# Sharing the last row of a ReLU-mean between two engines, with running sums and the scaling on GpSimd

## Chip, cores, metric

One core of a Trainium2 chip. The metric is the device time of one execution in microseconds; a profile's span is about 1.8 us shorter than that time (163.1 against 164.88 us for the kernel before).

## The reference

```python
x: float32 [32, 512, 1024]
out = np.mean(np.maximum(x, 0), axis=-1)      # float32 [32, 512]
```

67.1 MB are read and 64 KB written. Seen from the core, it is 128 partitions with 128 rows of 1024 values each.

## The kernel before

The rows are taken in eight tiles of 16 rows (8.4 MB each), three buffers deep. Even rows go to ScalarE, odd rows to VectorE. Each engine does ReLU and row sum in one instruction with an accumulator output; the profile lists the read-out of that accumulator as an instruction of its own (`DVE_READ_ACCUMULATOR` on VectorE). The last tile arrives in shrinking pieces (8, 4, 2, 1 rows, then row 15 of the tile in 512, 256 and 256 columns), so that little work is left after the last bytes. That tail is what the change rewrites:

```python
def dve_row(nc, src, acc):
    nc.vector.tensor_scalar(out=src, in0=src, scalar1=0.0, scalar2=None,
                            op0=ALU.max, op1=ALU.add, accum_out=acc)
...
def finish(lo, hi):                       # scaling by 1/1024
    nc.vector.tensor_scalar_mul(out=res[:, lo + 1:hi:2], in0=sum_v[:, lo + 1:hi:2], scalar1=inv)   # L73
    nc.scalar.mul(out=res[:, lo:hi:2], in_=sum_a[:, lo:hi:2], mul=inv)                             # L74
...
finish(0, j0)                             # 112 columns, before the last tile's rows
...                                       # rows 0 to 13 of the last tile
finish(j0, j0 + lo)                       # 14 columns
act_row(nc, xt[:, lo, :D // 2], part_a[:, 0:1])          # row 14, halves
dve_row(nc, xt[:, lo, D // 2:], part_v[:, 0:1])
act_row(nc, last[:, :D // 4], part_a[:, 1:2])            # row 15, first quarter
dve_row(nc, last[:, D // 4:D // 2], part_v[:, 1:2])      # second quarter
nc.vector.tensor_scalar(res[:, J - 2] = (part_a0 + part_v0) * inv)       # L106, row 14 (abridged)
dve_row(nc, last[:, D // 2:3 * D // 4], part_v[:, 2:3])  # third quarter
nc.vector.tensor_scalar(part_v1 = part_v1 + part_a1 + part_v2)           # L111 (abridged)
dve_row(nc, last[:, 3 * D // 4:], part_v[:, 3:4])        # last quarter
nc.vector.tensor_scalar(res[:, J - 1] = (part_v3 + part_v1) * inv)       # L116 (abridged)
nc.sync.dma_start(out=outr, in_=res)
```

In the compiled program, L106 stands ahead of the second quarter.

Of the kernel before, what the change touches and what calls it, by code (L numbers as in the profile page):

```python
# [1 line left out]

# [4 lines left out]

F32 = mybir.dt.float32
ALU = mybir.AluOpType
RELU = mybir.ActivationFunctionType.Relu  # L10


def act_row(nc, src, acc):

    nc.scalar.activation(out=src, in_=src, func=RELU, accum_out=acc)  # L15


def dve_row(nc, src, acc):

    nc.vector.tensor_scalar(  # L20
        out=src, in0=src, scalar1=0.0, scalar2=None,
        op0=ALU.max, op1=ALU.add, accum_out=acc,
    )


@with_exitstack
def kernel(
    ctx: ExitStack,
    tc: tile.TileContext,
    x: bass.AP,  # L30
    out: bass.AP,
):
    nc = tc.nc
    P = nc.NUM_PARTITIONS
    xf = x.flatten_outer_dims()
    R, D = xf.shape
    assert R % P == 0
    J = R // P
    inv = 1.0 / D
    xr = xf.rearrange("(p j) d -> p j d", p=P, j=J)  # L40
    outr = out.flatten().rearrange("(p j) -> p j", p=P, j=J)

    NB = 16
    BUFS = 3
    full = J // NB - 1

    row_pieces = []
    left = NB
    while left > 1:
        row_pieces.append(left // 2)  # L50
        left -= left // 2
    col_pieces = [D // 2, D // 4, D // 4]

    in_pool = ctx.enter_context(tc.tile_pool(name="in", bufs=BUFS))
    res_pool = ctx.enter_context(tc.tile_pool(name="res", bufs=1))
    sum_a = res_pool.tile([P, J], F32)
    sum_v = res_pool.tile([P, J], F32)
    res = res_pool.tile([P, J], F32)
    part_a = res_pool.tile([P, 2], F32)
    part_v = res_pool.tile([P, 4], F32)  # L60

    def rows(xt, lo, n, j0):

        for k in range(lo, lo + n):
            j = j0 + k
            if j % 2:
                dve_row(nc, xt[:, k, :], sum_v[:, j:j + 1])
            else:
                act_row(nc, xt[:, k, :], sum_a[:, j:j + 1])

    def finish(lo, hi):

        nc.vector.tensor_scalar_mul(out=res[:, lo + 1:hi:2], in0=sum_v[:, lo + 1:hi:2], scalar1=inv)  # L73
        nc.scalar.mul(out=res[:, lo:hi:2], in_=sum_a[:, lo:hi:2], mul=inv)  # L74

    for t in range(full):
        j0 = t * NB
        xt = in_pool.tile([P, NB, D], F32, name="xt")
        nc.sync.dma_start(out=xt, in_=xr[:, j0:j0 + NB, :])  # L79
        rows(xt, 0, NB, j0)  # L80

    j0 = full * NB
    xt = in_pool.tile([P, NB, D], F32, name="xt")
    lo = 0
    for n in row_pieces:
        nc.sync.dma_start(out=xt[:, lo:lo + n, :], in_=xr[:, j0 + lo:j0 + lo + n, :])  # L86
        lo += n
    c = 0
    for w in col_pieces:
        nc.sync.dma_start(out=xt[:, lo, c:c + w], in_=xr[:, j0 + lo, c:c + w])  # L90
        c += w

    finish(0, j0)
    lo = 0
    for n in row_pieces[:-1]:
        rows(xt, lo, n, j0)
        lo += n
    finish(j0, j0 + lo)


    last = xt[:, NB - 1, :]
    act_row(nc, xt[:, lo, :D // 2], part_a[:, 0:1])
    dve_row(nc, xt[:, lo, D // 2:], part_v[:, 0:1])
    act_row(nc, last[:, :D // 4], part_a[:, 1:2])
    dve_row(nc, last[:, D // 4:D // 2], part_v[:, 1:2])
    nc.vector.tensor_scalar(  # L106
        out=res[:, J - 2:J - 1], in0=part_a[:, 0:1], scalar1=part_v[:, 0:1], scalar2=inv,
        op0=ALU.add, op1=ALU.mult,
    )
    dve_row(nc, last[:, D // 2:3 * D // 4], part_v[:, 2:3])  # L110
    nc.vector.tensor_scalar(  # L111
        out=part_v[:, 1:2], in0=part_v[:, 1:2], scalar1=part_a[:, 1:2], scalar2=part_v[:, 2:3],
        op0=ALU.add, op1=ALU.add,
    )
    dve_row(nc, last[:, 3 * D // 4:], part_v[:, 3:4])
    nc.vector.tensor_scalar(  # L116
        out=res[:, J - 1:J], in0=part_v[:, 3:4], scalar1=part_v[:, 1:2], scalar2=inv,
        op0=ALU.add, op1=ALU.mult,
    )
    nc.sync.dma_start(out=outr, in_=res)  # L120


# [1 line left out]
_INS = ['x']  # L124
_OUTS = [((32, 512), 'float32')]


# [23 lines left out]
```

## Time and profile before

| | |
|---|---|
| time, median of 3 | 164.88 us (164.87 to 165.01) |
| span of the profile | 163.1 us |
| share of the chain that ended last | input transfers 83%, VectorE 14% |
| last landing of row 15's third piece | 159.19 us |
| issue of the output transfer | 160.67 us |
| between the two ("the stretch") | 1.48 us |
| issue to the end of the span | 2.43 us |

Up to the landing, the stream decides; after the issue, the output transfer and the program's close decide. A change of the tail can act only between the two. This kernel was profiled once, so its 1.48 us rest on one execution. The landings are read from the trace's records of the transfers' completion semaphores: the moment at which the last of sixteen increments arrives. The lines of the profile are shown in the prediction.

### The profile page before, as it was taken

To read this page: it belongs to the slowest core of one execution; us is meant where nothing else is said; L and a number is where in the kernel's file an instruction comes from. 1 tells how busy PE (TensorE), PEld (TensorE's weight loads), DVE (VectorE), ACT (ScalarE), POOL (GpSimd) and SP (SyncE) were. 2 spreads that over 40 slices of the span, in tenths; PEclk is the share of its full clock that TensorE was granted. 3 is DMA by queue.
4 is the path that set the end of the run, shared out by engine and by line. 5 is a ranking of instruction groups with operands and counts; after the bars stand their busy time and mean duration, and the time that the engine had idled before them with its cause. 6 is when DMAs were issued, how large, how long until landed. Compare 5 with 4: busy or idle time off the path is not lost.

```text
span 163.1 us, 351 instructions
## 1 busy us (share of the span) xinstructions
DVE 75.4 (46%) x139; ACT 69.4 (43%) x133; POOL 0.2 (0%) x4
## 2 busy tenths in 40 slices
DVE  0000039900596008940099202990059700799993
ACT  3000039700594008920099002980059500797890
POOL 0000000000000000000000000000000000000000
DMA  7979989989998998997997998998998897999970
GB/s 257 482 321 482 482 354 450 514 354 418 514 418 354 514 418 354 514 482 305 498 484 340 466 498 354 434 514 370 402 514 386 386 514 338 434 442 394 409 298 16
DMA packets 2162, 67.19 MB, mean 412 GB/s; under 512 B 240, under 2 KB 624, under 8 KB 880
## 3 DMA queue, kind: packets, MB, share of 16 engines
q1 hardware_dynamic: 2160, 67.18, 96.0%
q14 instruction: 2, 0.02, 0.0%
HBM read 67.11 MB, written 0.07 MB: 412 GB/s over the span
## 4 chain that ended last, share of the span: by engine, by line
DMA 83%; DVE 14%; SPq 1%; issue 0%; DVEq 0%
DMA xt<-in_x_dram 83%; DVE xt L20 13%; SPq L86 0%; SPq L79 0%; DVE part_v L111 0%; DVE res L116 0%; DVE res L106 0%; DVE res L73 0%; DVEq L20 0%; DVEq L111 0%; DVEq L106 0%
## 5 line engine op out<-in xcount | busy, mean ns | idle before, releaser
L20 DVE TENSOR_SCALAR_CACHE_REDUCE xt<-xt 128x1024 f32<-128x1024 f32 (+1 forms) x67 | 74.4, 1172 | 84.9 <-DMA xt<-in_x_dram 84.8
L15 ACT ACTIVATE xt<-xt 128x1024 f32<-128x1024 f32 (+1 forms) x65 | 66.7, 1027 | 88.9 <-DMA xt<-in_x_dram 88.9
L15 ACT ACTIVATION_READ_ACCUMULATOR xt<-xt 128x1 f32 x65 | 12.1, 187 | 0.0
L20 DVE DVE_READ_ACCUMULATOR xt<-xt 128x1 f32 x67 | 5.6, 83 | 0.0
L15 ACT ACT_TABLE_LOAD x1 | 1.3, 1283 | 0.7 <-PEq L135 0.7
L74 ACT ACTIVATE res<-sum_a 128x56 f32<-128x56 f32 (+1 forms) x2 | 0.5, 232 | 0.1
L73 DVE TENSOR_SCALAR res<-sum_v 128x56 f32<-128x56 f32 (+1 forms) x2 | 0.4, 184 | 0.1
L111 DVE TENSOR_SCALAR part_v<-part_v,part_a 128x1 f32<-128x1 f32 x1 | 0.3, 273 | 0.1
L106 DVE TENSOR_SCALAR res<-part_a,part_v 128x1 f32<-128x1 f32 x1 | 0.2, 214 | 0.1
L116 DVE TENSOR_SCALAR res<-part_v 128x1 f32<-128x1 f32 x1 | 0.2, 214 | 0.0
L135 POOL MEMSET const-uint8-127<- 128x1 uint8 x1 | 0.1, 102 | 0.0
L135 POOL MEMSET const-bfloat16-1.0<- 128x1 bf16 x1 | 0.1, 101 | 0.0
L135 POOL MEMSET const-float32-0.0<- 128x1 f32 x1 | 0.1, 98 | 0.2 <-issue 0.2
L135 POOL MEMSET const-float32-1.0<- 128x1 f32 x1 | 0.1, 98 | 0.0
## 6 DMA issues: line engine op xcount, KB each, us to landing
xt<-in_x_dram SPq DMA_DIRECT2D x1, 4096.0 KB, 39.0
xt<-in_x_dram SPq DMA_DIRECT2D x1, 2048.0 KB, 43.5
xt<-in_x_dram SPq DMA_DIRECT2D x1, 1024.0 KB, 45.5
xt<-in_x_dram SPq DMA_DIRECT2D x1, 512.0 KB, 46.3
xt<-in_x_dram SPq DMA_DIRECT2D x1, 256.0 KB, 46.5
xt<-in_x_dram SPq DMA_DIRECT2D x2, 128.0 KB, 42.7
xt<-in_x_dram SPq DMA_DIRECT2D x7, 48.9
out_dram<-res SPq DMA_DIRECT2D x1, 64.0 KB, 1.6
```

The lines of the kernel that those rows point to most:

```text
L15: nc.scalar.activation(out=src, in_=src, func=RELU, accum_out=acc)
L20: nc.vector.tensor_scalar(out=src, in0=src, scalar1=0.0, scalar2=None, op0=ALU.max, op1=ALU.add, accum_out=acc,)
L73: nc.vector.tensor_scalar_mul(out=res[:, lo + 1:hi:2], in0=sum_v[:, lo + 1:hi:2], scalar1=inv)
L74: nc.scalar.mul(out=res[:, lo:hi:2], in_=sum_a[:, lo:hi:2], mul=inv)
L106: nc.vector.tensor_scalar(out=res[:, J - 2:J - 1], in0=part_a[:, 0:1], scalar1=part_v[:, 0:1], scalar2=inv, op0=ALU.add, op1=ALU.mult,)
L111: nc.vector.tensor_scalar(out=part_v[:, 1:2], in0=part_v[:, 1:2], scalar1=part_a[:, 1:2], scalar2=part_v[:, 2:3], op0=ALU.add, op1=ALU.add,)
L116: nc.vector.tensor_scalar(out=res[:, J - 1:J], in0=part_v[:, 3:4], scalar1=part_v[:, 1:2], scalar2=inv, op0=ALU.add, op1=ALU.mult,)
L135: nc = _bacc.Bacc("TRN2", target_bir_lowering=False, num_devices=1)
```

## The change

Its intent: shorten what VectorE does after the last bytes. ScalarE gets half of the third quarter; VectorE's pieces of row 15 hand their sum on as the start value of the next; the scalings of finished rows and row 14's combination go to GpSimd.

```diff
-def dve_row(nc, src, acc):
+def dve_row(nc, src, acc, init=None):
-        out=src, in0=src, scalar1=0.0, scalar2=None,
+        out=src, in0=src, scalar1=0.0, scalar2=init,
...                                    # one tile `sums` in place of sum_a, sum_v; one tile `part`
     def finish(lo, hi):
-        nc.vector.tensor_scalar_mul(out=res[:, lo + 1:hi:2], in0=sum_v[:, lo + 1:hi:2], scalar1=inv)
-        nc.scalar.mul(out=res[:, lo:hi:2], in_=sum_a[:, lo:hi:2], mul=inv)
+        nc.gpsimd.tensor_scalar(
+            out=res[:, lo:hi], in0=sums[:, lo:hi], scalar1=inv, scalar2=0.0, op0=ALU.mult, op1=ALU.add,
+        )
...
+    nc.gpsimd.tensor_scalar(            # L98: row 14's combination, was L106 on VectorE
+        out=res[:, J - 2:J - 1], in0=part[:, 0:1], scalar1=part[:, 1:2], scalar2=inv, op0=ALU.add, op1=ALU.mult,
+    )
+    act_row(nc, last[:, :256], part[:, 2:3])
+    dve_row(nc, last[:, 256:512], part[:, 3:4])
+    nc.gpsimd.tensor_scalar(            # L103
+        out=part[:, 4:5], in0=part[:, 2:3], scalar1=inv, scalar2=0.0, op0=ALU.mult, op1=ALU.add,
+    )
+    act_row(nc, last[:, 512:640], part[:, 5:6])
+    dve_row(nc, last[:, 640:768], part[:, 6:7], init=part[:, 3:4])
+    nc.scalar.activation(               # L108
+        out=part[:, 7:8], in_=part[:, 5:6], func=ACT.Identity, scale=inv, bias=part[:, 4:5],
+    )
+    dve_row(nc, last[:, 768:], part[:, 8:9], init=part[:, 6:7])
+    nc.vector.scalar_tensor_tensor(     # L112
+        out=res[:, J - 1:J], in0=part[:, 8:9], scalar=inv, in1=part[:, 7:8], op0=ALU.mult, op1=ALU.add,
+    )
```

More of the change, by code (lines that the diff above doesn't have):

```diff
@@ L9 @@
 ALU = mybir.AluOpType
-RELU = mybir.ActivationFunctionType.Relu
+ACT = mybir.ActivationFunctionType
 def act_row(nc, src, acc):
-    nc.scalar.activation(out=src, in_=src, func=RELU, accum_out=acc)
-def dve_row(nc, src, acc):
+    nc.scalar.activation(out=src, in_=src, func=ACT.Relu, accum_out=acc)
+def dve_row(nc, src, acc, init=None):
     nc.vector.tensor_scalar(
-        out=src, in0=src, scalar1=0.0, scalar2=None,
+        out=src, in0=src, scalar1=0.0, scalar2=init,
         op0=ALU.max, op1=ALU.add, accum_out=acc,
@@ L41 @@
     outr = out.flatten().rearrange("(p j) -> p j", p=P, j=J)
+    xlast = xr[:, J - 1, :]
     NB = 16
-    BUFS = 3
     full = J // NB - 1
-    row_pieces = []
-    left = NB
-    while left > 1:
-        row_pieces.append(left // 2)
-        left -= left // 2
-    col_pieces = [D // 2, D // 4, D // 4]
-    in_pool = ctx.enter_context(tc.tile_pool(name="in", bufs=BUFS))
+    row_pieces = [8, 4, 2, 1]
+    assert sum(row_pieces) == NB - 1
+    col_pieces = [512, 256, 256]
+    assert sum(col_pieces) == D
+    in_pool = ctx.enter_context(tc.tile_pool(name="in", bufs=3))
     res_pool = ctx.enter_context(tc.tile_pool(name="res", bufs=1))
-    sum_a = res_pool.tile([P, J], F32)
-    sum_v = res_pool.tile([P, J], F32)
+    sums = res_pool.tile([P, J], F32)
     res = res_pool.tile([P, J], F32)
-    part_a = res_pool.tile([P, 2], F32)
-    part_v = res_pool.tile([P, 4], F32)
+    part = res_pool.tile([P, 10], F32)
     def rows(xt, lo, n, j0):
@@ L65, in rows @@
             j = j0 + k
-            if j % 2:
-                dve_row(nc, xt[:, k, :], sum_v[:, j:j + 1])
-            else:
-                act_row(nc, xt[:, k, :], sum_a[:, j:j + 1])
+            (dve_row if j % 2 else act_row)(nc, xt[:, k, :], sums[:, j:j + 1])
     def finish(lo, hi):
-        nc.vector.tensor_scalar_mul(out=res[:, lo + 1:hi:2], in0=sum_v[:, lo + 1:hi:2], scalar1=inv)
-        nc.scalar.mul(out=res[:, lo:hi:2], in_=sum_a[:, lo:hi:2], mul=inv)
+        nc.gpsimd.tensor_scalar(
+            out=res[:, lo:hi], in0=sums[:, lo:hi], scalar1=inv, scalar2=0.0, op0=ALU.mult, op1=ALU.add,
+        )
     for t in range(full):
@@ L83 @@
     xt = in_pool.tile([P, NB, D], F32, name="xt")
+    prev, last = xt[:, NB - 2, :], xt[:, NB - 1, :]
     lo = 0
@@ L89 @@
     for w in col_pieces:
-        nc.sync.dma_start(out=xt[:, lo, c:c + w], in_=xr[:, j0 + lo, c:c + w])
+        nc.sync.dma_start(out=last[:, c:c + w], in_=xlast[:, c:c + w])
         c += w
@@ L98 @@
     finish(j0, j0 + lo)
-    last = xt[:, NB - 1, :]
-    act_row(nc, xt[:, lo, :D // 2], part_a[:, 0:1])
-    dve_row(nc, xt[:, lo, D // 2:], part_v[:, 0:1])
-    act_row(nc, last[:, :D // 4], part_a[:, 1:2])
-    dve_row(nc, last[:, D // 4:D // 2], part_v[:, 1:2])
-    nc.vector.tensor_scalar(
-        out=res[:, J - 2:J - 1], in0=part_a[:, 0:1], scalar1=part_v[:, 0:1], scalar2=inv,
-        op0=ALU.add, op1=ALU.mult,
-    )
-    dve_row(nc, last[:, D // 2:3 * D // 4], part_v[:, 2:3])
-    nc.vector.tensor_scalar(
-        out=part_v[:, 1:2], in0=part_v[:, 1:2], scalar1=part_a[:, 1:2], scalar2=part_v[:, 2:3],
-        op0=ALU.add, op1=ALU.add,
-    )
-    dve_row(nc, last[:, 3 * D // 4:], part_v[:, 3:4])
-    nc.vector.tensor_scalar(
-        out=res[:, J - 1:J], in0=part_v[:, 3:4], scalar1=part_v[:, 1:2], scalar2=inv,
-        op0=ALU.add, op1=ALU.mult,
+    act_row(nc, prev[:, :512], part[:, 0:1])
+    dve_row(nc, prev[:, 512:], part[:, 1:2])
+    nc.gpsimd.tensor_scalar(
+        out=res[:, J - 2:J - 1], in0=part[:, 0:1], scalar1=part[:, 1:2], scalar2=inv, op0=ALU.add, op1=ALU.mult,
+    )
+    act_row(nc, last[:, :256], part[:, 2:3])
+    dve_row(nc, last[:, 256:512], part[:, 3:4])
+    nc.gpsimd.tensor_scalar(
+        out=part[:, 4:5], in0=part[:, 2:3], scalar1=inv, scalar2=0.0, op0=ALU.mult, op1=ALU.add,
+    )
+    act_row(nc, last[:, 512:640], part[:, 5:6])
[6 more added lines that the diff above has]
+        out=res[:, J - 1:J], in0=part[:, 8:9], scalar=inv, in1=part[:, 7:8], op0=ALU.mult, op1=ALU.add,
     )
```

## The prediction

> **What bounds the kernel now.** I read the page first, then the chain that ended last, then the timeline of the last 7 us, then the trace's records of when each transfer's completion semaphore reached its full count. The page's chain and groups say that the kernel is a stream from HBM with a short tail of compute:
>
> ```profile
> DMA 83%; DVE 14%; SPq 1%; issue 0%; DVEq 0%
> ...
> HBM read 67.11 MB, written 0.07 MB: 412 GB/s over the span
> ...
> L20 DVE TENSOR_SCALAR_CACHE_REDUCE xt<-xt 128x1024 f32<-128x1024 f32 (+1 forms) x67 | 74.4, 1172 | 84.9 <-DMA xt<-in_x_dram 84.8
> L15 ACT ACTIVATE xt<-xt 128x1024 f32<-128x1024 f32 (+1 forms) x65 | 66.7, 1027 | 88.9 <-DMA xt<-in_x_dram 88.9
> ```
>
> Both compute engines are idle for more than half the span, and that idle time ends on input transfers. The 13% of "DVE xt L20" in the chain is mostly two batches of 16 instructions (42.54 and 100.93 us, 9.22 us each) through which a buffer came free; transfers of other buffers run beside them, so it is not lost stream time. The input is 67.1 MB whatever the program does, and the change leaves every input transfer and its order alone. So only what follows the last bytes can move. The timeline of the end, in start, duration, engine, line:
>
> ```profile
> 156.62 1.22 DVE L20 TENSOR_SCALAR_CACHE_REDUCE xt<-xt 128x1024 f32<-128x1024 f32 x1
> ...
> 157.88 0.17 DVE L73 TENSOR_SCALAR res<-sum_v 128x7 f32<-128x7 f32 x1
> 157.91 0.63 ACT L15 ACTIVATE xt<-xt 128x512 f32<-128x512 f32 x1
> 157.96 0.68 DVE L20 TENSOR_SCALAR_CACHE_REDUCE xt<-xt 128x512 f32<-128x512 f32 x1
> ...
> 158.75 0.21 DVE L106 TENSOR_SCALAR res<-part_a,part_v 128x1 f32<-128x1 f32 x1
> 158.87 0.19 ACT L15 ACTIVATION_READ_ACCUMULATOR xt<-xt 128x1 f32 x1
> 158.88 0.41 DVE L20 TENSOR_SCALAR_CACHE_REDUCE xt<-xt 128x256 f32<-128x256 f32 x1
> 159.22 0.08 DVE L20 DVE_READ_ACCUMULATOR xt<-xt 128x1 f32 x1
> 159.22 0.42 DVE L20 TENSOR_SCALAR_CACHE_REDUCE xt<-xt 128x256 f32<-128x256 f32 x1
> 159.56 0.08 DVE L20 DVE_READ_ACCUMULATOR xt<-xt 128x1 f32 x1
> 159.75 0.27 DVE L111 TENSOR_SCALAR part_v<-part_v,part_a 128x1 f32<-128x1 f32 x1
> 159.94 0.41 DVE L20 TENSOR_SCALAR_CACHE_REDUCE xt<-xt 128x256 f32<-128x256 f32 x1
> 160.27 0.08 DVE L20 DVE_READ_ACCUMULATOR xt<-xt 128x1 f32 x1
> 160.39 0.21 DVE L116 TENSOR_SCALAR res<-part_v 128x1 f32<-128x1 f32 x1
> 160.67 0.35 SPq L120 DMA_DIRECT2D out_dram<-res  x1
> ```
>
> ScalarE is done at 159.06 (158.87 + 0.19); VectorE works alone for another 1.54 us, to 160.60. The semaphore records give the landings: two-row piece 156.59, row 14 at 157.89, the three pieces of row 15 at 158.53, 158.87 and 159.19 us. So 1.48 us lie between the last landing and the issue of the output. The output itself (1.6 us to landing) stays as it is.
>
> **What the Trainium skill says.** "VectorE: DVE Perf Modes", section "The DRAIN you can't avoid": a statistic that the next Vector instruction reads as its scalar needs a semaphore between them, and the page measured such semaphores to cost nothing in a series of copies. This trace differs for accumulators: without a dependency the next reduction starts together with the accumulator read (159.22 and 159.22), while L116, with one wait, starts 0.04 us after that read's end (160.35 to 160.39), and L106 and L111, which need two waits, 0.11 us after it (158.64 to 158.75, 159.64 to 159.75). "ScalarE: Activation LUTs", section "What ACT_TABLE_LOAD costs": 0.833 ns per element, a table load of about 1283 ns, about 93 ns for each pointer operand. The trace agrees on two: (1043 - 627)/512 = 0.81 ns, and one load of 1283 ns. Its section "Table sets" puts identity in every set, and the compiled program does have a single load. "GPSIMD Engine Reference", section 3.1: some 2.6 cycles at 1.2 GHz per element, and 4497 ns for a two-input add of 2048 elements; that leaves about 60 ns of fixed cost, my estimate. No arithmetic on GpSimd is in this trace, only memsets of 0.10 us. "SBUF — State Buffer", section "Who interferes with whom": a `tensor_scalar` that also writes its accumulator does not take the port pair that VectorE shares with GpSimd. The trace has (1216 - 679)/512 = 1.05 ns per element for it, one element per cycle, which fits; so I expect no blocking.
>
> **The change part by part.** The compiled programs show every row of the bulk on the same engine and with the same waits on transfers, so I carry nothing over from there. The 56-column scalings on both engines (0.25 and 0.20 us at 148 us) go to GpSimd as one of 112 columns; they lay before a transfer that landed at 149.2 and were worth nothing. In the tail I walk VectorE from 156.62 us, with intervals from the timeline: 1.14 us for 1024 columns, 0.60 for 512, 0.34 for 256 (start to next start), by the slope 0.205 for 128. A pointer scalar I put at 0.04 us (L116 with one, 214 ns, against the scaling of seven columns with none, 174 ns).
>
> 1. The 7-column scaling (L73) goes. Its slot could be used from 157.76, but row 14 lands only at 157.89: the half row starts at 157.92 instead of 157.96. Gain 0.04.
> 2. L106 goes to GpSimd. The 256-column piece may start at 157.92 + 0.60 = 158.52; its data lands at 158.53, so 158.55 instead of 158.88. Gain now 0.33.
> 3. The 128-column piece is seeded with the sum just made. It waits for the accumulator read (158.55 + 0.34 + 0.08 = 158.97), and one separate wait (the transfer) is already met at 158.87: start 158.97 + 0.04 = 159.01. Its accumulator is read at 159.01 + 0.205 + 0.04 = 159.255 to 159.335.
> 4. The last 256 columns, seeded again: start 159.375 (data from 159.19), accumulator read from 159.755 to 159.835. In before, this stood at 160.35, so the gain is 0.515: 128 columns fewer (0.135), L111 with its waits gone, and the two seeds paid for.
> 5. The final combination now needs ScalarE as well, thus two waits: 159.835 + 0.11 = 159.945, plus 0.21 (as L116) = 160.155. The issue follows 0.07 later, as before (160.60 to 160.67): 160.225 against 160.67. **Gain 0.445 us.**
>
> ScalarE beside it: the first 256 columns run as now (read out by 159.06). The added 128 columns start at 158.97, last 0.31 by slope with the read-out overlapping (0.19), done at about 159.37. The identity has two waits, from 159.47, and lasts 0.21 + 0.09 = 0.30: 159.77, which is 0.06 ahead of VectorE's 159.835. GpSimd gets its operand at 159.06, so it has until about 159.45, that is 0.39 us from semaphore to semaphore for one column; its earlier one-column operation needs to be done by 159.1 after inputs at 158.64. By the estimate above one such operation is 0.06 us plus a wake-up that I can't read off anywhere. I take this as hidden with little to spare, and spoil the sum by 0.03: 0.42. Thus 164.88 - 0.42 = 164.46 us.
>
> **Rivals.** *GpSimd becomes the last to finish.* For it: its result is in series between two ScalarE instructions, it also has the 14-column scaling and row 14's result in its strict order, and no profile line gives its latency. Every 0.1 us above 0.39 us would cost 0.1 us; with 0.8 us per operation, three in a row from 157.9 end at 160.3, the identity at 160.7, the combination at about 161.0, issue at 161.1: 165.3 us. Against it: the memsets of 0.10 us and the page's small fixed part.
> *A library load at GpSimd.* The compiled program has an extra GpSimd instruction ahead of its first arithmetic that selects a code library. The GPSIMD page (section 2.1) gives about 6 us for a first call. It sits behind no wait, and even if the load came at the first scaling, 148 us, it would be over by 154 and the next need is at 157.8: hidden, 164.5 us. Should it lengthen the launch itself outside the span, some us could come on top (for instance 168 to 171); I see no sign of a wait of other engines on it.
> *Landings swallow the gain.* If the last two pieces landed later, VectorE would wait. The last landing (159.19) is 0.19 us ahead of need (159.375), and the records are from one run; a stream 0.3 us later gives back only 0.1. That makes 164.55. A faster tail can't move the stream: all input transfers are issued by 120.5 us.
> *Seeds cost more than 0.04 us.* Two of them lie on the path; if a pointer costs 0.1 each, 0.12 is lost: 164.6.
>
> **Range and chances.** The kernel's three runs lie within 0.14 us, the gain can hardly pass 0.65 us (the seeds free and the final waits 0.04), and the GpSimd rival with middling latencies takes all of the gain. Range 164.15 to 165.0. Two per cent is 3.3 us, more than the whole stretch from last landing to output issue, so faster by that much is next to excluded; slower needs GpSimd operations of over 1.5 us or a load that is not hidden.
>
> **What would show it.** Right: bulk unchanged, row 15's pieces landing as now to within 0.2 us, VectorE's five tail instructions at 157.9, 158.55, 159.0, 159.4 and 159.9, the chain's last part on VectorE, output issue near 160.2. Wrong: VectorE idle ahead of the final combination with ScalarE's identity as releaser, and behind that GpSimd (then the GpSimd step was mis-sized); VectorE idle ahead of a seeded piece for more than 0.05 us, or such a piece much over 0.32 and 0.45 us (seeds mis-sized); a time that grows while the output issue comes earlier (a cost outside the span); a shifted landing of the last piece (the stream was not as untouched as I claim).

## The result and the profile after

| | before | after |
|---|---|---|
| time, median | 164.94 us (4 runs, 164.87 to 165.21) | 164.44 us (4 runs, 164.37 to 164.78) |
| ratio, 95% interval | | 0.9971 (0.9953 to 0.9989) |
| last landing | 159.19 us | 159.11 us |
| issue of the output | 160.67 us | 160.15 us |
| stretch | 1.48 us | 1.04 us |
| issue to the end of the span | 2.43 us | 2.44 us |

A ratio is the mean time of one kernel's fast runs over that of the other's of the same rounds, so it is not quite the ratio of the medians.

The page of the changed kernel: chain and groups. The last group is GpSimd's scaling, with idle time and releaser at the end of the line.

```profile
DMA 84%; DVE 13%; SPq 1%; issue 0%; DVEq 0%
...
L15 ACT ACTIVATE xt<-xt 128x1024 f32<-128x1024 f32 (+1 forms) x66 | 67.0, 1016 | 89.2 <-DMA xt<-in_x_dram 89.2
...
L65 POOL TENSOR_SCALAR res<-sums 128x112 f32<-128x112 f32 (+1 forms) x2 | 0.5, 252 | 157.2 <-DVE xt L20 157.2
```

The picture of the whole has not moved: a stream with a tail. ScalarE has one accumulating instruction more. GpSimd's two scalings cost 0.25 us each on an engine that had nothing to do.

The timeline of the changed kernel's end (start, duration, engine, line):

```profile
157.83 0.69 DVE L20 TENSOR_SCALAR_CACHE_REDUCE xt<-xt 128x512 f32<-128x512 f32 x1
...
158.47 0.42 DVE L20 TENSOR_SCALAR_CACHE_REDUCE xt<-xt 128x256 f32<-128x256 f32 x1
...
158.79 0.19 ACT L15 ACTIVATION_READ_ACCUMULATOR xt<-xt 128x1 f32 x1
...
158.93 0.35 DVE L20 TENSOR_SCALAR_CACHE_REDUCE xt<-xt,part 128x128 f32<-128x128 f32 x1
159.06 0.19 POOL L103 TENSOR_SCALAR part<-part 128x1 f32<-128x1 f32 x1
...
159.21 0.08 DVE L20 DVE_READ_ACCUMULATOR xt<-xt,part 128x1 f32 x1
159.32 0.48 DVE L20 TENSOR_SCALAR_CACHE_REDUCE xt<-xt,part 128x256 f32<-128x256 f32 x1
159.36 0.29 ACT L108 ACTIVATE part<-part 128x1 f32<-128x1 f32 x1
159.73 0.08 DVE L20 DVE_READ_ACCUMULATOR xt<-xt,part 128x1 f32 x1
159.92 0.16 DVE L112 SCALAR_TENSOR_TENSOR res<-part 128x1 f32<-128x1 f32 x1
160.15 0.35 SPq L115 DMA_DIRECT2D out_dram<-res  x1
```

The half row starts 0.02 us after row 14 lands (157.81), the 256-column piece 0.02 after its own landing (158.45). From there on no VectorE instruction waits for data; each seeded piece follows the end of the read-out before it by 0.03 to 0.04 us, and the combination by 0.11 (159.81 to 159.92). GpSimd starts 0.08 us after ScalarE's read-out (158.98 to 159.06) and takes 0.19. ScalarE's identity is over at 159.65, well before VectorE's read-out at 159.81. So the final wait is VectorE's own, as predicted.

Of the 0.52 us by which the issue came earlier in this pair of profiles, 0.08 is an earlier landing, which is not the change's doing, and 0.44 is the stretch.

### The profile page after: what moved, and what is told of

Same layout as the page of the kernel before. It is cut to its first block, busy times and chain, and to the rows that moved or that the text cites. A ratio compares the mean times of both kernels' runs of the same rounds, so it can differ in the third digit from the quotient of the medians.

```text
span 162.6 us, 358 instructions
## 1 busy us (share of the span) xinstructions
DVE 74.8 (46%) x135; ACT 69.6 (43%) x134; POOL 1.2 (1%) x8
## 4 chain that ended last, share of the span: by engine, by line
DMA 84%; DVE 13%; SPq 1%; issue 0%; DVEq 0%
DMA xt<-in_x_dram 84%; DVE xt L20 13%; SPq L80 1%; SPq L72 0%; DVE res L112 0%; DVEq L20 0%; DVEq L112 0%
## 5 line engine op out<-in xcount | busy, mean ns | idle before, releaser
L65 POOL TENSOR_SCALAR res<-sums 128x112 f32<-128x112 f32 (+1 forms) x2 | 0.5, 252 | 157.2 <-DVE xt L20 157.2
L20 DVE TENSOR_SCALAR_CACHE_REDUCE xt<-xt,part 128x128 f32<-128x128 f32 (+1 forms) x2 | 0.8, 412 | 0.1
L98 POOL TENSOR_SCALAR res<-part 128x1 f32<-128x1 f32 x1 | 0.3, 264 | 0.6 <-ACT xt L15 0.6
L103 POOL TENSOR_SCALAR part<-part 128x1 f32<-128x1 f32 x1 | 0.2, 191 | 0.1
```

The lines of the kernel that those rows point to most:

```text
L65: nc.gpsimd.tensor_scalar(out=res[:, lo:hi], in0=sums[:, lo:hi], scalar1=inv, scalar2=0.0, op0=ALU.mult, op1=ALU.add,)
L98: nc.gpsimd.tensor_scalar(out=res[:, J - 2:J - 1], in0=part[:, 0:1], scalar1=part[:, 1:2], scalar2=inv, op0=ALU.add, op1=ALU.mult,)
L103: nc.gpsimd.tensor_scalar(out=part[:, 4:5], in0=part[:, 2:3], scalar1=inv, scalar2=0.0, op0=ALU.mult, op1=ALU.add,)
```

## The experiments

The theory: VectorE's own chain of dependent instructions between the landings of row 15 and the output's issue sets the end, and the stretch measures it. Rival A: sharing and seeding are the gain, the scaling was hidden anyway. Rival B: chance in the stream. Rival C: the chain through GpSimd and ScalarE's identity is what counts.

| run | last landing, us | stretch, us | time, us (runs) | ratio to before, 95% interval |
|---|---|---|---|---|
| e1_only_scaling | 159.63 | 1.17 | 164.87 (4) | 0.9995 (0.9978 to 1.0011) |
| e6_only_scaling_again | 159.45 | 1.16 | 164.81 (6) | 0.9981 (0.9969 to 0.9993) |
| e2_scaling_back | 159.14 | 1.32 | 164.87 (4) | 0.9997 (0.9982 to 1.0012) |
| e10_row14_back | 159.33 | 1.32 | 164.97 (4) | 1.0000 (0.9987 to 1.0014) |
| e3_no_share | 159.32 | 1.16 | 164.65 (4) | 0.9983 (0.9968 to 0.9998) |
| e9_no_seeds | 159.49 | 1.19 | 164.80 (4) | 0.9987 (0.9973 to 1.0000) |
| e8_gpsimd_chain | 159.24 | 1.56 | 165.16 (4) | 1.0000 (0.9985 to 1.0016) |
| e4_floor (wrong result) | 159.33 | 0.24 | 163.77 (4) | 0.9934 (0.9920 to 0.9949) |
| e5_changed_again | 159.73 | 1.03 | 164.72 (5) | 0.9979 (0.9967 to 0.9991) |
| e12_changed_third | 159.34 | 1.04 | 164.52 (5) | 0.9974 (0.9960 to 0.9987) |
| e7_lean_128 | 159.34 | 0.80 | 164.50 (6) | 0.9970 (0.9956 to 0.9985) |
| e11_lean_again | 159.25 | 0.80 | 164.25 (5) | 0.9957 (0.9945 to 0.9970) |

Landing and stretch are of the one profiled execution, the time is the median of all.

The stretch can be split once more in the traces. The end of VectorE's last read-out, counted from the last landing, was 1.17 us in before, 0.86 in e1, 0.86 in e3 and 0.71 in the changed kernel. So the work moved to GpSimd took 0.31 us off VectorE's chain, the seeds in place of L111 nothing, and the sharing 0.15. What follows (wait, combination, issue) became 0.02 longer, from 0.31 to 0.33 us. Unrounded, 0.467 less 0.022 gives the 0.445.

### e1: scaling and row 14's combination to GpSimd, nothing else

```diff
 # kernel before
...                                    # ScalarE's row sums go into sum_v too, sum_a is dropped
-        nc.vector.tensor_scalar_mul(...); nc.scalar.mul(...)
+        nc.gpsimd.tensor_scalar(out=res[:, lo:hi], in0=sum_v[:, lo:hi], scalar1=inv, scalar2=0.0, ...)
-    nc.vector.tensor_scalar(out=res[:, J - 2:J - 1], ...)
+    nc.gpsimd.tensor_scalar(out=res[:, J - 2:J - 1], ...)
```

> The kernel before, with the scaling and row 14's combination moved to GpSimd and nothing else. I read each run by the stretch from the landing of the last input piece to the issue of the output: 1.48 us in the kernel before, 1.04 us in the changed one. Theory (VectorE's chain of dependent instructions sets that stretch, and taking the combination out of it is most of the gain): the stretch is 1.48 - 0.33 = 1.15 us, time 0.33 us below before. Rival A (the gain comes from sharing and seeding in row 15, and the scaling was hidden anyway): 1.45 us. Rival B (the changed kernel was only lucky with the stream): stretch unchanged at 1.48 us.

The stretch is 1.17 us, where the theory said 1.15. The timeline of this run shows how the two quarters now follow one another on VectorE without the combination between them:

```profile
158.99 0.42 DVE L20 TENSOR_SCALAR_CACHE_REDUCE xt<-xt 128x256 f32<-128x256 f32 x1
159.22 0.27 POOL L106 TENSOR_SCALAR res<-part_a,part_v 128x1 f32<-128x1 f32 x1 [0.56 <-ACT xt L15]
...
159.34 0.42 DVE L20 TENSOR_SCALAR_CACHE_REDUCE xt<-xt 128x256 f32<-128x256 f32 x1
```

But the time was only 0.05 us below before, and not the 0.33. The profile shows a landing 0.44 us later than before's. Whether that was chance or this kernel's own stream had to be tried (e6, with e5 beside it, below).

### e2: the scalings and row 14's combination back

```diff
 # changed kernel
-        nc.gpsimd.tensor_scalar(out=res[:, lo:hi], in0=sums[:, lo:hi], ...)
+        nc.vector.tensor_scalar_mul(out=res[:, lo + 1:hi:2], in0=sums[:, lo + 1:hi:2], scalar1=inv)
+        nc.scalar.mul(out=res[:, lo:hi:2], in_=sums[:, lo:hi:2], mul=inv)
-    nc.gpsimd.tensor_scalar(out=res[:, J - 2:J - 1], ...)
+    nc.vector.tensor_scalar(out=res[:, J - 2:J - 1], ...)
```

> The changed kernel, with the scalings back on VectorE and ScalarE and row 14's combination back on VectorE; sharing and seeds stay. Theory: every VectorE instruction after the half row is 0.33 us later, stretch 1.04 + 0.33 = 1.37 us, so that sharing and seeds alone are worth about 0.11 us against 1.48. Rival A (sharing and seeding are the gain): 1.05 to 1.1 us. Rival B: no change that exceeds 0.05 us from the changed kernel.

The stretch is 1.32 us: 0.28 us come back of the 0.33 expected. On VectorE's chain it is 0.32: the last read-out ends 1.03 us after the landing, against 0.71. The rest is made up at the output's issue, which here follows the combination by 0.03 us instead of 0.06 (lines under e10). Rival A falls, since sharing and seeding alone leave 1.32 of 1.48 us. Rival B falls too: with a landing (159.14) next to that of the changed kernel (159.11) the issue came 0.31 us later.

### e10: only row 14's combination back

```diff
 # changed kernel
-    nc.gpsimd.tensor_scalar(out=res[:, J - 2:J - 1], ...)
+    nc.vector.tensor_scalar(out=res[:, J - 2:J - 1], ...)
```

> The changed kernel with only row 14's combination back on VectorE; the scalings stay on GpSimd. It divides what the second experiment undid together (stretch 1.32 us). Theory (row 14's landing, not the scaling, sets when the half row starts, so the scaling's removal is worth at most 0.04 us): stretch 1.28 to 1.32 us. If the scaling was worth more than that: 1.1 to 1.2 us.

1.32 us, equal to e2. So of the parts that went to GpSimd, the combination of row 14 is worth 0.28 us. The scalings come out as nothing, but as the sum of two effects. The last combination and the issue in e2, then in e10:

```profile
160.28 0.16 DVE L111 SCALAR_TENSOR_TENSOR res<-part 128x1 f32<-128x1 f32 x1
160.46 0.35 SPq L114 DMA_DIRECT2D out_dram<-res  x1
...
160.43 0.16 DVE L112 SCALAR_TENSOR_TENSOR res<-part 128x1 f32<-128x1 f32 x1
160.65 0.35 SPq L115 DMA_DIRECT2D out_dram<-res  x1
```

With the scaling on VectorE (e2) the half row starts 0.08 us after row 14's landing, without it (e10) 0.02, and at VectorE's last read-out e10 is still 0.05 us ahead (0.98 against 1.03 us after the last landing). But in e10 the issue follows the combination's end by 0.06 us, in e2 by 0.03. The traces show the difference: in e2 and e3 (no other run) the output's issue waits for VectorE's semaphore itself; elsewhere it waits for GpSimd's (in before, ScalarE's), and a wait instruction of its own for VectorE's stands in front. So in this arrangement scaling on GpSimd gains 0.05 us on VectorE and gives nearly all of it back at the output. With row 14's combination on GpSimd as well, the scaling was not tried by itself.

### e3: the third quarter on VectorE alone

```diff
 # changed kernel
-    act_row(nc, last[:, 512:640], part[:, 5:6])
-    dve_row(nc, last[:, 640:768], part[:, 6:7], init=part[:, 3:4])
-    nc.scalar.activation(out=part[:, 7:8], in_=part[:, 5:6], func=ACT.Identity, scale=inv, bias=part[:, 4:5])
+    dve_row(nc, last[:, 512:768], part[:, 6:7], init=part[:, 3:4])
-        out=res[:, J - 1:J], in0=part[:, 8:9], scalar=inv, in1=part[:, 7:8], ...
+        out=res[:, J - 1:J], in0=part[:, 8:9], scalar=inv, in1=part[:, 4:5], ...
```

> The changed kernel, with the third quarter of row 15 on VectorE alone (256 columns seeded, not 128 on each engine); ScalarE's identity goes. Theory: 128 more columns on VectorE's chain at 1.05 ns, 0.135 us: stretch 1.18 us. Rival A (sharing is the main part): 1.35 us or more. Rival C (GpSimd and ScalarE's identity are what the final combination waits for): stretch no longer than 1.04 us, since the identity is gone.

1.16 us, 0.12 more than the changed kernel; on VectorE's chain 0.15 (read-out 0.86 against 0.71 us after the landing), of which the quicker issue of this run (0.03 against 0.06 us) hides 0.03. Sharing 128 columns is worth that. Rival C does not fit: without the identity the stretch got longer, not shorter. Since VectorE has more to do here, e8 has to settle it. This run also isolates the seeds: up to the last read-out it differs from e1 on VectorE by seeds instead of L111, and has 0.86 us as e1 has. Two seeds cost what the separate sum L111 cost; by themselves they gain nothing.

### e9: no seeds, the sums folded by GpSimd

```diff
 # changed kernel
-        out=part[:, 4:5], in0=part[:, 2:3], scalar1=inv, scalar2=0.0, op0=ALU.mult, op1=ALU.add,
+        out=part[:, 4:5], in0=part[:, 2:3], scalar1=part[:, 3:4], scalar2=inv, op0=ALU.add, op1=ALU.mult,
-    dve_row(nc, last[:, 640:768], part[:, 6:7], init=part[:, 3:4])
+    dve_row(nc, last[:, 640:768], part[:, 6:7])
+    nc.gpsimd.tensor_scalar(
+        out=part[:, 9:10], in0=part[:, 6:7], scalar1=inv, scalar2=part[:, 4:5], op0=ALU.mult, op1=ALU.add,
+    )
-        ..., scale=inv, bias=part[:, 4:5],
+        ..., scale=inv, bias=part[:, 9:10],
-    dve_row(nc, last[:, 768:], part[:, 8:9], init=part[:, 6:7])
+    dve_row(nc, last[:, 768:], part[:, 8:9])
```

> The changed kernel without running sums: each VectorE piece of row 15 makes its own sum, and two GpSimd instructions in series fold the first two into the bias of ScalarE's identity. VectorE is then freed of its own waits: its last read-out should end 0.03 + 0.34 + 0.08 = 0.45 us after the last landing (0.70 in the changed kernel). But GpSimd's second instruction ends about 0.44 us after the landing, the identity about 0.8, the combination and issue follow. Theory (a chain across engines replaces VectorE's): stretch 1.0 to 1.1 us, with VectorE idle before the combination for 0.3 us and ScalarE as releaser. Rival A (seeds are the gain, without them it is lost): stretch 1.2 us or more. If freeing VectorE alone counted: 0.8 us.

1.19 us: above my 1.0 to 1.1, and just below Rival A's 1.2. The timeline of this run, with the idle time and its releaser in brackets:

```profile
159.46 0.27 POOL L103 TENSOR_SCALAR part<-part 128x1 f32<-128x1 f32 x1
...
159.83 0.27 POOL L108 TENSOR_SCALAR part<-part 128x1 f32<-128x1 f32 x1
159.86 0.08 DVE L20 DVE_READ_ACCUMULATOR xt<-xt 128x1 f32 x1
160.13 0.29 ACT L111 ACTIVATE part<-part 128x1 f32<-128x1 f32 x1 [0.48 <-POOL part L108]
160.46 0.16 DVE L115 SCALAR_TENSOR_TENSOR res<-part 128x1 f32<-128x1 f32 x1 [0.52 <-ACT part L111]
```

VectorE is read out at 159.94, 0.45 us after the landing, exactly as expected. Then it idles for 0.52 us on ScalarE, which had waited for GpSimd. What I mis-sized is GpSimd: an instruction with pointer scalars takes 0.27 us (0.19 without), and the second starts 0.11 us after the end of the first. (In e8's series, with one wait each, GpSimd's instructions start 0.27 us apart.) The mechanism that I named holds, with a longer chain across engines. The use of the seeds is thus to keep the sum on one engine while the other takes columns.

### e8: three more GpSimd instructions in series

```diff
 # changed kernel, L103
+    for _ in range(2):
+        nc.gpsimd.tensor_scalar(out=part[:, 9:10], in0=part[:, 9:10], scalar1=1.0, scalar2=0.0, ...)
+    nc.gpsimd.tensor_scalar(out=part[:, 4:5], in0=part[:, 9:10], scalar1=1.0, scalar2=0.0, ...)
```

(L103 itself writes column 9 here.)

> The changed kernel with three more GpSimd instructions in series before ScalarE's identity, each waiting for the one before. In the changed kernel the identity ends about 0.2 us ahead of the wait that VectorE's final combination ends. Each instruction with its wait should take 0.19 + 0.08 to 0.15 us, so the identity comes 0.8 to 1.0 us later. Theory (slack of 0.2 us, then the bound moves to GpSimd): stretch 1.04 + 0.6 to 0.8, that is 1.65 to 1.85 us. Rival C (GpSimd already sets the end): 1.85 to 2.05 us. Rival B (tail doesn't matter): no change.

```profile
159.20 0.19 POOL L103 TENSOR_SCALAR part<-part 128x1 f32<-128x1 f32 x1
...
160.02 0.19 POOL L110 TENSOR_SCALAR part<-part 128x1 f32<-128x1 f32 x1
160.25 0.29 ACT L115 ACTIVATE part<-part 128x1 f32<-128x1 f32 x1 [0.84 <-POOL part L110]
160.57 0.16 DVE L119 SCALAR_TENSOR_TENSOR res<-part 128x1 f32<-128x1 f32 x1 [0.63 <-ACT part L115]
```

Three more instructions moved the last GpSimd start by 0.82 us, 0.27 each with the wait. The identity started 1.01 us after the last landing, against 0.26 in the changed kernel: 0.75 later. The stretch grew by 0.52 only. So the path through GpSimd had 0.23 us of slack, and Rival C is wrong for the changed kernel. The stretch (1.56) is under my range (1.65 to 1.85), since I had counted 0.2 us of slack and up to 0.34 us per instruction.

### e4: what is left to gain

```diff
 # changed kernel: all of row 15's instructions replaced (wrong on purpose)
+    nc.vector.tensor_scalar_mul(out=res[:, J - 1:J], in0=last[:, D - 1:D], scalar1=inv)
```

> Wrong result on purpose: of row 15 one element only is scaled and written, after the landing of the last piece; everything else is as in the changed kernel. It gives what any arrangement of the tail could still gain. Theory: landing to instruction 0.03, the instruction 0.2, to the issue 0.07: stretch 0.3 us, time about 164.44 - 0.74 = 163.7 us. Rival B (something other than the tail, for instance the close of the program, holds the end): time falls by less than 0.4 us.

```profile
159.35 0.15 DVE L101 TENSOR_SCALAR res<-xt 128x1 f32<-128x1 f32 x1 [0.61 <-DMA xt<-in_x_dram]
159.56 0.35 SPq L102 DMA_DIRECT2D out_dram<-res  x1
```

A stretch of 0.24 us: 0.02 to the instruction, 0.15 for it, 0.07 to the issue. The time fell to 163.77 us, where 163.7 was expected. With these transfers, little more than this can be gained by arranging the compute of the tail: even the kernel before is within 0.7% of that.

### e6, e5, e12: the same kernels again

No edit: e6 is e1's kernel, e5 and e12 are the changed kernel.

> The first experiment once more, since its stretch was 1.17 us (0.31 below before, as the theory said) while its time was only 0.05 us below before, with a landing 0.44 us later than before's. If that landing was chance: stretch 1.17 us again, landing nearer 159.2 us, and a time some 0.3 us below before. If the kernel's stream is really slower: landing again near 159.6 us and again no gain.

> The changed kernel once more, unaltered. So far its profile had the last input piece land at 159.11 us; four other kernels with the same input transfers had 159.14 to 159.63 us, so the stream ends up to 0.5 us apart between executions. If the stretch from that landing to the issue of the output is the kernel's own and the landing is chance: stretch 1.04 us again, to within 0.05, wherever the landing is, and time 0.3 to 0.5 us below before. If the landing is the kernel's own: landing again below 159.2 us.

> The changed kernel a third time, beside the shorter version of the same call: stretch 1.03 us to within 0.02, time 0.4 us below before and 0.2 above the shorter version.

Stretches of 1.16, 1.03 and 1.04 us agree with 1.17 and 1.04 of the first runs to 0.02 us. The landings do not agree: the changed kernel had 159.11, 159.73 and 159.34 us in its three profiles. So the stretch belongs to the kernel, and the landing moves by 0.6 us from one execution to another with identical transfers; what moves it is not shown. In e1's kernel too the landing did not stay late: its second set of runs gave a ratio of 0.9981, about the 0.998 that 0.32 us of 165 amount to. The runs without a profile can be placed by an estimate: in all 14 profiles the time less landing and stretch is 4.21 to 4.23 us. By that, e1's four runs had landings at 159.4 to 159.6 us and the seven of before beside them at 159.1 to 159.3; e6 had 159.2 to 159.7, before 159.2 to 159.8. So e1 drew late streams in one call and not in the other. It also means that four runs of a kernel do not measure 0.2 us; the profile's stretch does. The changed kernel's three ratios are 0.9971, 0.9979 and 0.9974, that is 0.35 to 0.48 us, around the 0.445 of the stretch.

### e7 and e11: a shorter tail

VectorE takes the first 512 columns, ScalarE 384 with the scaling inside its ReLU, VectorE the last 128 seeded with its first sum. No GpSimd and no identity in row 15, one seed instead of two.

```diff
 # changed kernel
-    col_pieces = [512, 256, 256]
+    col_pieces = [512, 384, 128]
...                                    # row 15's instructions replaced by
+    dve_row(nc, last[:, :512], part[:, 3:4])
+    nc.scalar.activation(out=last[:, 512:896], in_=last[:, 512:896], func=ACT.Relu, scale=inv, accum_out=part[:, 4:5])
+    dve_row(nc, last[:, 896:], part[:, 6:7], init=part[:, 3:4])
+    nc.vector.scalar_tensor_tensor(
+        out=res[:, J - 1:J], in0=part[:, 6:7], scalar=inv, in1=part[:, 4:5], op0=ALU.mult, op1=ALU.add)
```

> A version that should beat both: row 15 arrives as 512, 384 and 128 columns. VectorE takes the first 512, ScalarE the 384 (it scales by 1/1024 in the same instruction), VectorE the last 128 seeded with its first sum, then one combination; GpSimd and the identity have no part in row 15. Theory: VectorE's half of 512 columns is read out about 0.03 us before the last landing, so the seeded piece starts 0.06 after the landing, its read-out ends 0.205 + 0.07 + 0.08 later, then 0.11 for two waits, 0.16 for the combination, 0.07 to the issue: stretch 0.75 us, time about 0.3 us below the changed kernel. ScalarE must be read out by then: 384 columns from 0.15 before the landing take 0.43 + 0.19 us, so it comes 0.03 us after VectorE at most. Rival C (dependent waits across engines cost more than within one): stretch 0.95 us or more. Rival: the smaller last piece lands later and eats the gain.

> The seventh experiment once more, for its time: stretch was 0.80 us against 1.03 to 1.04 us of the changed kernel, but landings wander by up to 0.5 us between executions. Theory: stretch again 0.80 us to within 0.03, time 0.2 us below the changed kernel of the same call, 0.6 below before. If the smaller last piece makes landings later: landing near 159.7 us and no gain over the changed kernel.

The timeline of the second of these runs:

```profile
158.60 0.69 DVE L20 TENSOR_SCALAR_CACHE_REDUCE xt<-xt 128x512 f32<-128x512 f32 x1
...
159.08 0.52 ACT L102 ACTIVATE xt<-xt 128x384 f32<-128x384 f32 x1 [0.40 <-DMA xt<-in_x_dram]
159.21 0.08 DVE L20 DVE_READ_ACCUMULATOR xt<-xt 128x1 f32 x1
159.36 0.35 DVE L20 TENSOR_SCALAR_CACHE_REDUCE xt<-xt,part 128x128 f32<-128x128 f32 x1
...
159.82 0.16 DVE L106 SCALAR_TENSOR_TENSOR res<-part 128x1 f32<-128x1 f32 x1
```

Stretch 0.80 us twice, results correct. I had expected 0.75: the seeded piece starts 0.07 after the read-out (159.29 to 159.36) and 0.11 after the landing, not 0.06. The likely reason is in the trace: its wait for the transfer is an instruction of its own, which here ends together with the read-out (both about 0.05 us after the landing); in the changed kernel, where that wait was over at least 0.05 us before the read-out's end, the piece followed by 0.03. The smaller last piece did not land later (159.34 and 159.25 us). The ratios are 0.9970 and 0.9957. In the second the changed kernel beside it had 0.9974, so the shorter version was 0.27 us faster by the medians (164.25 against 164.52); in the first it was 0.22 us (164.50 against 164.72). The intervals of the two kernels overlap; it is the stretch, 0.80 against 1.03 to 1.04, that separates them. It is the fastest correct kernel of this study.

## Why the prediction was right, point by point

- **The number.** 164.46 predicted, 164.44 measured. The agreement to 0.02 us is luck: four runs of the changed kernel lie 0.4 us apart, and the interval of the ratio allows a gain of 0.2 to 0.8 us. What was tested is the stretch.
- **The bound.** Right. The stream is untouched, and the gain is bounded by the stretch. The floor run shows the remainder. (The greatest gain, by the terms that I named for it, is 0.445 + 0.08 for free seeds + 0.07 for shorter waits, or 0.60, and not 0.65.)
- **Step 1, the 7-column scaling: 0.04 us.** Right at its place: the half row starts 0.02 us after row 14's landing instead of 0.07. In the stretch it does not show by itself: e10 equals e2, since what is gained on VectorE is lost at the issue (see e10).
- **Step 2, L106 to GpSimd: 0.33 in all.** At the 256-column piece exactly that: it starts 0.64 us before the last landing instead of 0.30. In the stretch, together with the scalings, 0.31 forward (1.48 to 1.17) and 0.28 backward (1.32 to 1.04). The backward figure is smaller by the quicker issue of e2.
- **Steps 3 and 4, seeds.** The two seeded pieces started 0.08 and 0.05 us before the times given, with landings 0.07 to 0.08 us earlier than in before; counted from the last landing, right to within 0.03 us. The seed was mis-sized: I put 0.04 us for the pointer; the 128-column piece took 346 ns with it and 285 ns without (e9), and the 256-column piece 479 against 420 ns, so 0.06 each. The last read-out ended 0.71 us after the last landing, where these steps give 0.65.
- **Step 5, the combination: 0.21 us.** It took 0.16. This error of 0.05 and the one of some 0.05 at the last read-out cancel, so the sum of 0.445 us agrees with the measured 0.445 (1.485 to 1.040) better than its terms deserve.
- **GpSimd hidden.** Right, with more room than I gave it: ScalarE's identity ended 0.15 us ahead of VectorE's read-out where I worked out 0.06, and e8 shows 0.23 us until it would have delayed the end. The operation took 0.19 us, three times my estimate of 0.06, and with its wake-up 0.27 of the 0.39 allowed. No blocking showed: the 256-column piece took 0.42 us with GpSimd's L98 beside it, 0.41 to 0.42 in before. With nothing to be spoilt, the 0.03 that I took off was needless.
- **The library load.** It cost nothing that shows. The trace has two `MODIFY_POOL_CONFIG` instructions on GpSimd at 0.74 and 0.77 us, 148 us before the first scaling. That scaling started 0.18 us after the last of its inputs and took 0.29 us; issue to the span's end is unchanged (2.44 against 2.43 us), and so is time less span (1.8 us).
- **Rival "landings swallow the gain".** The case that I named, the last two pieces late by themselves, did not occur: in all runs with this cut of row 15 the third piece landed 0.30 to 0.32 us after the second. What occurred is that the whole tail of the stream came later, and that leaves the stretch as it is (1.03 us with the landing at 159.73), so the issue moves with the landing and not by a third of it. I underrated how far the landing moves between executions; it is the same size as the gain.

## What to carry to other kernels

When a stream bounds a kernel, measure a change of its tail from the last landing to the output's issue in the trace: that stretch repeated to 0.02 us here while the landing moved by 0.6. In such a tail, count dependencies rather than columns: taking one small combination off VectorE was worth 0.3 us and halving 256 columns 0.12 to 0.15, while swapping a separate sum for running sums changed nothing by itself. Hand small work to another engine only where nothing waits for it soon; two such hops in series (e9) cost more than the engine that they relieved had saved. And look at which of two waits comes last: in the changed kernel's combination it was the one that stands in front as an instruction of its own (VectorE's read-out), and the start came 0.11 us after it; in e8 and e9 it was the other (ScalarE's identity), and the start came 0.03 us after it.

## What the Trainium skill lacked or had wrong

- "VectorE: DVE Perf Modes", section "The DRAIN you can't avoid", finds for copies that a semaphore between Vector instructions costs nothing extra. That does not carry over to the accumulating instructions here: without a wait the next one starts with the read-out (e1: 159.34 and 159.34), with one wait 0.03 to 0.04 us after the read-out's end, a combination with two waits 0.11 us after it when the read-out comes last. With the read-out's 0.08 us, such a dependency costs 0.12 to 0.19 us.
- "GPSIMD Engine Reference", section 3.1, has rates per element and no latency of small instructions. Here one column took 0.19 us, with pointer scalars 0.26 to 0.27, 112 columns 0.29; it started 0.08 us after its input with one wait, 0.10 to 0.18 with two; a series with single waits ran at 0.27 us per instruction (e8).
- In none of the pages that I used did I find the cost of a pointer as start value of an accumulating `tensor_scalar` (0.06 us), or how much the end of a 67 MB stream varies between executions of one kernel (159.11 to 159.73 us).
